# Layer A's sums of squares in a two-layer encoder: the additions move from GpSimd to VectorE

## The chip, the core and the metric

The kernel runs on one core of one Trainium2 chip. A core has five engines with instruction queues of their own: TensorE (PE in the profile; PEld is its weight load), VectorE (DVE), ScalarE (ACT), GpSimd (POOL) and SyncE (SP, which issues transfers here). They share an on-chip memory of 128 partitions and wait for each other by semaphores. The metric is the device time of one execution in microseconds (us); less is better.

## The reference

Two encoder layers on 512 tokens of width 1024, all in float32. Layer A is attention in three dilated windows, layer B attention in a two-dimensional neighbourhood. Cut to what matters:

```python
def rms_norm(x, g):
    y = x * lax.rsqrt(jnp.mean(x * x, axis=-1, keepdims=True) + RMS_EPS)
    return y * g

def reference(x, norm_gain, ...):
    for i in range(2):                       # layer A, then layer B
        hn = rms_norm(x, norm_gain[i])
        y = mixer_a(hn, ...) if i == 0 else mixer_b(hn, ...)
        x = x + y

def mixer_a(hn, w_in, w_out, ...):           # mixer_b has the same frame
    proj = hn @ w_in                         # q, k, v of each head group, and a gate
    ...                                      # attention
    return (y * silu(gate)) @ w_out
```

The change touches one step of this: the mean of `x * x` over the 1024 features of each token, in layer A's `rms_norm`.

## The kernel before, in words

**Layout.** x is held turned over, features on partitions: `x_all` is 8 blocks of 128 features x 512 tokens. The sum of squares over the features of a token therefore has two steps: the eight squared blocks are added, element by element, into one tile `ssq` (128 x 512), and a matmul with a column of ones (`row_sums`, tile `pk`) adds over the partitions.

**Matmuls in three parts.** A float32 product is made of three matmuls in a faster 32-bit format. Each operand is split into a high half, rounded, and a low half, the rest. For a weight, `cast` makes `wh` on ScalarE from the loaded `wraw`, and `rest` makes `wl` = `wraw` - `wh` on VectorE or GpSimd; among the first weights all of these subtractions go to VectorE. For x, `norm` makes `hn_h` on ScalarE and `hn_l` on VectorE, for each of the eight blocks. `mm3` issues the three matmuls, with `hn_h` x `wh`, `hn_h` x `wl`, `hn_l` x `wh` in this order.

**The beginning.** The first projection of layer A (`project`, eight steps k, each of four token blocks by three matmuls) uses x times its gain alone; the division by each token's root mean square, which needs `ssq`, is put in later as a scale of the results. So while TensorE works through the eight steps, block by block, ScalarE and VectorE make `hn_h`, `hn_l`, `wh` and `wl` for each step, ScalarE squares each block (`square_a`: block 0 straight into `ssq`, blocks 1 to 7 into tiles `sqx`, four of them in turn), and GpSimd adds the seven `sqx` to `ssq`, one after the other. After the first projection come the four small matmuls of `row_sums`, a reciprocal root on VectorE into `rs_n`, and `spread`, which hands it to all partitions (tile `pa`); then x itself is scaled (`scale_x`) and split anew (`renorm`, odd blocks on GpSimd), and sums and differences of its blocks are made for later products (`mix`, tiles `mixed`, `mix_h`, `mix_l`).

**Layer B** has the same step in `square_b`, where the additions are made by VectorE.

**The order of the work.** TensorE's order is that in which the program is traced, and it is written by hand: a generator `main` issues the large products, a generator `side` the rest (`square_a` and `row_sums` among them), and `run` interleaves them by an estimate of the matmuls' time. The other engines' queues are ordered by a planner that simulates the program, except where an instruction is pinned to the traced order. The engines' wrapper `Ordered` pins all of them while `held[0]` is set; it is set from the end of the second projection (some 54 us into the span) to the last attention step of layer A. So the beginning, with the change in it, and most of layer B are the planner's. Each engine runs its own queue strictly in that order: an instruction that waits holds up those behind it.

The functions that the diff touches, and what calls them:

Of the kernel before, what the change touches and what calls it, by code (L numbers as in the profile page):

```python
# [46 lines left out]
def tile_hybrid_encoder(  # L47
# [49 lines left out]
    vec, act, pol, syn = (Ordered(e) for e in (nc.vector, nc.scalar, nc.gpsimd, nc.sync))  # L97
# [407 lines left out]
    def square_a(k):  # L505
        if k == 0:
            st["ssq"] = wk.tile([P, S], F32, tag="eg", name="ssq", bufs=1)
        sq = wk.tile([P, 512], F32, tag="p", name="sqx", bufs=PB) if k else st["ssq"]
        act.activation(sq, x_all[:, k, :], AF.Square)
        if k:  # L510
            pol.tensor_add(st["ssq"], st["ssq"], sq)

    def scale_x():

# [82 lines left out]
    st = {}  # L597
# [807 lines left out]
    def side():  # L1405
        for k in range(KT):
            norm(0, k, x_all[:, k, :])
            if k:
                square_a(k - 1)
            stamp["na", k] = 0  # L1410
            yield 1000
        square_a(KT - 1)
        yield 8000
        row_scale(row_sums(st.pop("ssq")))
# [120 lines left out]
```

## Time and profile before

| | |
|---|---|
| median of 3 runs | 846.02 us (844.99 to 846.65) |
| profiled execution, its own time | 846.23 us |
| its span, from the first to the last instruction | 844.3 us |
| granted TensorE clock, mean | 1.000 |
| PE / DVE / ACT / POOL busy | 827.9 / 632.8 / 507.7 / 292.0 us |
| moved by DMA | 131.97 MB, mean 156 GB/s |

In the rows of the profile, L85 is the line of the wrapper `Ordered`, through which nearly every instruction of VectorE, ScalarE and GpSimd is issued, and L324 that of `matmul`; operations are therefore told apart by their tiles, written `out<-in`. A row of the order of time gives the start and the length in us, the engine, the instruction, its tiles and shape, how many equal neighbours are merged in the row, and in brackets the idle time of the engine before it and what ended that. The length of merged rows runs from the start of the first to the end of the last.

### The profile page before, as it was taken

Reading aid. Unit: us, or ns where it says so; the run is one execution under the profiler, and the core shown is the slowest. Engines: PE = TensorE matmul, PEld = TensorE weight load, DVE = VectorE, ACT = ScalarE, POOL = GpSimd, SP = SyncE. Lnnn points to the kernel's source line nnn. Section 1 sums busy time; section 2 is a strip of 40 time slices with the busy share of each in tenths; the row PEclk is TensorE's granted clock in tenths of the full one; section 3 lists DMA queues with packets and bytes.
Section 4 is the critical chain, followed back from the end, with each engine's and each line's share of the span. In section 5 each row is a group of like instructions: output and inputs, shape, how many; then the busy total and the mean of one; then the engine's idle time right before and its main releaser. Section 6 shows DMA issues by size and latency. Waiting matters only on the chain.

```text
span 844.3 us, 18126 instructions
## 1 busy us (share of the span) xinstructions
PE 827.9 (98%) x6611; PEld 684.9 (81%) x6611; DVE 632.8 (75%) x1653; ACT 507.7 (60%) x1066; POOL 292.0 (35%) x259
## 2 busy tenths in 40 slices
PE   8999999999999999999999999999999999999998
PEld 6877878878877878878888887789998898889786
DVE  7899997897996886896796876466668767776742
ACT  7657766846846846747747738454546664666440
POOL 5042343543533533533533524213123222322201
PEclk9999999999999999999999999999999999999999
DMA  9426765676687776785676554473265456634212
GB/s 339 144 57 165 194 154 150 141 168 197 133 181 211 159 174 173 164 210 134 157 180 176 105 183 144 152 235 114 91 191 164 130 145 180 179 129 114 85 51 101
DMA packets 56169, 131.97 MB, mean 156 GB/s; under 512 B 7184, under 2 KB 24528, under 8 KB 55952
## 3 DMA queue, kind: packets, MB, share of 16 engines
q1 hardware_dynamic: 49456, 108.39, 41.8%
q0 software_dynamic: 6048, 22.02, 15.2%
q8 instruction: 52, 0.85, 0.4%
q10 hardware_dynamic: 576, 0.41, 0.2%
q14 instruction: 37, 0.30, 0.1%
HBM read 111.73 MB, written 11.72 MB: 146 GB/s over the span
## 4 chain that ended last, share of the span: by engine, by line
PE 76%; ACT 9%; DVE 8%; issue 3%; DMA 3%; POOL 1%; SPq 0%; DVEq 0%; ACTq 0%; POOLq 0%
PE acc L324 63%; PE log L324 5%; PE o L324 4%; ACT p L85 4%; PE tp L328 3%; DVE wl L85 2%; ACT wh L85 1%; DVE na L85 1%; DMA wraw<-in_w 1%; DVE rawq L85 1%; DMA yr<-y_d 1%; ACT rawk L85 1%; DVE gt L85 1%; DVE p L85 1%; DMA pt<-in_xt 1%
## 5 line engine op out<-in xcount | busy, mean ns | idle before, releaser
L85 POOL TENSOR_TENSOR wl<-wraw,wh 128x512 fp32r<-128x512 f32 (+1 forms) x153 | 198.2, 1296 | 434.5 <-PE acc L324 223.2
L85 ACT CAST wh<-wraw 128x512 fp32r<-128x512 f32 (+1 forms) x360 | 209.3, 593 | 194.1 <-PE acc L324 154.9
L85 DVE TENSOR_TENSOR wl<-wraw,wh 128x512 fp32r<-128x512 f32 (+1 forms) x207 | 158.3, 768 | 44.5 <-PE acc L324 33.4
L324 PE MATMUL acc<-wh,hn_h 128*128 128x384 f32 (+1 forms) x488 | 185.5, 380 | 2.9 <-DVE gt L85 1.7
L324 PE MATMUL acc<-wl,hn_h 128*128 128x384 f32 (+1 forms) x488 | 177.2, 363 | 3.1 <-DVE wl L85 3.1
L324 PE MATMUL acc<-wh,hn_l 128*128 128x384 f32 (+1 forms) x488 | 176.9, 362 | 0.0
L85 ACT ACTIVATE p<-p,mn 128x256 f32<-128x256 f32 (+2 forms) x248 | 137.6, 584 | 32.3 <-DVE mn L85 32.3
L324 PEld LDWEIGHTS acc<-wh,hn_h 128*128 128x128 f32 x488 | 91.7, 188 | 21.4 <-issue 7.0
L324 PEld LDWEIGHTS acc<-wl,hn_h 128*128 128x128 f32 x488 | 91.9, 188 | 12.1 <-DVE wl L85 4.9
L324 PEld LDWEIGHTS acc<-wh,hn_l 128*128 128x128 f32 x488 | 91.6, 188 | 9.5
L324 PE MATMUL acc<-wh,mix_h 128*128 128x512 f32 x224 | 89.2, 398 | 0.0
L324 PE MATMUL acc<-wl,mix_h 128*128 128x512 f32 x224 | 87.6, 391 | 0.0
L324 PE MATMUL acc<-wh,mix_l 128*128 128x512 f32 x224 | 87.4, 390 | 0.0
L324 PE MATMUL acc<-hn_h,wh 128*128 128x512 f32 x192 | 79.0, 412 | 0.3 <-ACT rawb L85 0.2
L324 PE MATMUL acc<-hn_h,wl 128*128 128x512 f32 x192 | 75.1, 391 | 0.0
L324 PE MATMUL acc<-hn_l,wh 128*128 128x512 f32 x192 | 75.0, 391 | 0.0
L85 DVE STREAM_TRANSPOSE pt<-p 128x512 f32<-128x512 f32 (+1 forms) x60 | 40.6, 687 | 23.7 <-ACT p L85 23.6
L85 DVE TENSOR_REDUCE ss<-sq 128x4 f32<-128x256 f32 (+1 forms) x96 | 46.1, 501 | 11.0 <-POOL sq L85 5.9
L324 PE MATMUL acc<-y_h,wh 128*128 128x512 f32 x128 | 51.9, 406 | 0.5 <-ACT gt L85 0.5
L324 PEld LDWEIGHTS acc<-wh,mix_h 128*128 128x128 f32 x224 | 42.1, 188 | 10.0 <-issue 1.6
L324 PE MATMUL acc<-y_h,wl 128*128 128x512 f32 x128 | 50.0, 391 | 0.0
L324 PE MATMUL acc<-y_l,wh 128*128 128x512 f32 x128 | 49.9, 390 | 0.0
(148 smaller groups left out, 1361.5 us busy)
## 6 DMA issues: line engine op xcount, KB each, us to landing
wraw<-in_w SPq DMA_DIRECT2D x95, 512.0 KB
wraw<-in_w POOLq DMA_DIRECT2D x42, 512.0 KB, 7.0
wraw<-in_w SPq DMA_DIRECT2D x38, 384.0 KB
pt<-pt SPq DMA_DIRECT2D x106, 64.0 KB
td<-tr SPq DMA_DIRECT2D x24, 224.0 KB
pt<-td SPq DMA_DIRECT2D x24, 224.0 KB
e<-l_d SPq DMA_DIRECT2D x32, 112.0 KB
e<-l_d SPq DMA_DIRECT2D x16, 128.0 KB
```

The costliest lines, as they stand in the source:

```text
L85: m = f(*args, **kw)
L324: nc.tensor.matmul(o, l, r, **kw)
L328: nc.tensor.transpose(o, i, ident)
```

## The change

The addition of each squared block to `ssq` is issued on VectorE instead of GpSimd, seven times in all, on tiles of 128 x 512 in float32. Squares, tiles and the matmuls that read `ssq` stay as they are.

```diff
     def square_a(k):
         if k == 0:
             st["ssq"] = wk.tile([P, S], F32, tag="eg", name="ssq", bufs=1)
         sq = wk.tile([P, 512], F32, tag="p", name="sqx", bufs=PB) if k else st["ssq"]
         act.activation(sq, x_all[:, k, :], AF.Square)
         if k:
-            pol.tensor_add(st["ssq"], st["ssq"], sq)
+            vec.tensor_add(st["ssq"], st["ssq"], sq)
```

## The prediction

> **What bounds the kernel now.** I read the page first, then what TensorE waits for, then busy time by stretch, and last the order of time of each engine around the seven additions. From the page, the span, two engines' busy time and the chain that ended last:
>
> ```profile
> span 844.3 us, 18126 instructions
> PE 827.9 (98%) x6611; PEld 684.9 (81%) x6611; DVE 632.8 (75%) x1653; ACT 507.7 (60%) x1066; POOL 292.0 (35%) x259
> PE 76%; ACT 9%; DVE 8%; issue 3%; DMA 3%; POOL 1%; SPq 0%; DVEq 0%; ACTq 0%; POOLq 0%
> ```
>
> TensorE (PE) is busy for 98% of the span and carries 76% of the chain. So the time is the length of a matmul stream in a fixed order, plus the places where it stands still, and an edit on another engine counts only where it opens or closes such a place. The view of who waited for whom, TensorE's rows, names the largest kind (columns: us in total, times, longest):
>
> ```profile
> PE acc L324 <- DVE wl L85: 3.1, 3, 1.3
> ```
>
> `wl` is the low half of a weight, which VectorE (DVE) makes. Where these waits fall, and what VectorE and GpSimd (POOL) do there, is told by the busy time in three stretches (columns: stretch, its length, then busy us of PE, PEld, DVE, ACT, POOL with counts, granted clock, DMA share, GB/s):
>
> ```profile
> 8.40:20.70 12.30, 11.24 (x48) 8.42 (x47) 11.98 (x9) 11.08 (x20) 10.63 (x7) 1.00 1.03 410
> 20.70:27.00 6.30, 6.30 (x29) 5.22 (x28) 4.99 (x8) 1.25 (x2) 0.01 (x1) 1.00 0.79 238
> 27.00:54.00 27.00, 27.00 (x126) 21.42 (x126) 24.32 (x52) 16.72 (x29) 6.39 (x5) 1.00 0.38 100
> ```
>
> In the first stretch, where the additions run, VectorE is busy for 11.98 of 12.30 us with only 9 instructions; in the second, with GpSimd silent, it makes 8 in 4.99. The clock is 1.00 in all three. The two engines in order of time (start, length, instruction, count; neighbours of one kind are merged):
>
> ```profile
> 7.28 0.75 DVE L85 SCALAR_TENSOR_TENSOR hn_l<-pt,ng,hn_h 128x512 fp32r<-128x512 f32 x1 [0.41 <-ACT hn_h L85]
> 8.31 1.43 DVE L85 TENSOR_TENSOR wl<-wraw,wh 128x512 fp32r<-128x512 f32 x1 [0.28 <-ACT wh L85]
> 9.66 1.40 DVE L85 SCALAR_TENSOR_TENSOR hn_l<-pt,ng,hn_h 128x512 fp32r<-128x512 f32 x2
> 11.38 3.09 DVE L85 TENSOR_TENSOR wl<-wraw,wh 128x512 fp32r<-128x512 f32 x2 [0.32 <-ACT wh L85]
> 14.39 3.48 DVE L85 SCALAR_TENSOR_TENSOR hn_l<-pt,ng,hn_h 128x512 fp32r<-128x512 f32 x2
> 17.80 3.46 DVE L85 TENSOR_TENSOR wl<-wraw,wh 128x512 fp32r<-128x512 f32 x2
> 21.19 1.40 DVE L85 SCALAR_TENSOR_TENSOR hn_l<-pt,ng,hn_h 128x512 fp32r<-128x512 f32 x2
> 22.51 3.23 DVE L85 TENSOR_TENSOR wl<-wraw,wh 128x512 fp32r<-128x512 f32 x5
> ```
>
> ```profile
> 7.84 1.34 POOL L85 TENSOR_TENSOR ssq<-ssq,sqx 128x512 f32<-128x512 f32 x1 [6.53 <-ACT sqx L85]
> 10.46 10.25 POOL L85 TENSOR_TENSOR ssq<-ssq,sqx 128x512 f32<-128x512 f32 x6 [1.27 <-ACT sqx L85]
> 38.45 1.31 POOL L85 TENSOR_TENSOR hn_l<-pt,hn_h 128x512 fp32r<-128x512 f32 x1 [17.74 <-ACT hn_h L85]
> ```
>
> This is the heart of the case. The same `wl` operation costs 3.23 / 5 = 0.65 us after 22.51 and 3.46 / 2 = 1.73 us at 17.80. `hn_l` costs 1.40 / 2 = 0.70 us at 9.66 and 21.19, and 3.48 / 2 = 1.74 us at 14.39. The slow ones lie exactly where GpSimd's six additions lie, 10.46 to 20.71, and those come every 10.25 / 6 = 1.71 us, against 1.31 us for a GpSimd operation of that size at 38.45. The two engines step in turn, one operation each per 1.7 us. What that does to TensorE is in its own rows:
>
> ```profile
> 9.54 0.39 PE L324 MATMUL acc<-wh,hn_h 128*128 128x512 f32 x1
> 9.79 0.50 PE L324 MATMUL acc<-wl,hn_h 128*128 128x512 f32 x1
> 10.13 0.40 PE L324 MATMUL acc<-wh,hn_l 128*128 128x512 f32 x1
> ...
> 12.46 0.39 PE L324 MATMUL acc<-wh,hn_h 128*128 128x512 f32 x1
> 12.83 0.50 PE L324 MATMUL acc<-wl,hn_h 128*128 128x512 f32 x1
> 13.16 0.39 PE L324 MATMUL acc<-wh,hn_l 128*128 128x512 f32 x1
> 13.39 0.40 PE L324 MATMUL acc<-wh,hn_h 128*128 128x512 f32 x1
> ...
> 17.95 0.39 PE L324 MATMUL acc<-wh,hn_l 128*128 128x512 f32 x1
> 18.18 0.39 PE L324 MATMUL acc<-wh,hn_h 128*128 128x512 f32 x1
> 19.63 0.50 PE L324 MATMUL acc<-wl,hn_h 128*128 128x512 f32 x1 [1.06 <-DVE wl L85]
> 19.97 0.40 PE L324 MATMUL acc<-wh,hn_l 128*128 128x512 f32 x1
> ```
>
> Undisturbed, matmuls start 0.23 us apart (17.95 to 18.18, 13.16 to 13.39). Three times the one that first reads a new `wl` starts late: by 0.02 at 9.79, 0.14 at 12.83 and 1.22 at 19.63. After each the next comes 0.33 to 0.34 us on, 0.10 to 0.11 more than usual, so a halt costs a tenth on top. The three together: 0.02 + 0.14 + 1.22 + 3 x 0.11 = 1.7 us.
>
> **Taken away: seven additions on GpSimd.** They cost nothing directly, since nobody waits for GpSimd here; what goes is the slowing of VectorE. Over the seven VectorE operations that ran slow (one from 8.31, two each from 11.38, 14.39 and 17.80) that is 1.43 + 3.09 + 3.48 + 3.46 = 11.46 us, against five at 0.65 and two at 0.70 = 4.65 us: 6.8 us of VectorE's time.
>
> **Added: seven additions on VectorE.** This operation stands in the trace, since layer B adds its squares on VectorE already (min/median/max ns):
>
> ```profile
> L85 DVE TENSOR_TENSOR ssq<-ssq,sqx x7: 676/681/884, 569.2 to 576.5; 128x512 f32<-128x512 f32 x7
> ```
>
> Bounds: 0.65 us apiece by the row at 22.51, 0.88 by this row's longest. I take 0.68, the median: 7 x 0.68 = 4.8 us. So VectorE is left 6.8 - 4.8 = 2.0 us ahead when the stretch ends, while doing more.
>
> The additions are new waits in VectorE's queue: each waits for a square from ScalarE (ACT), and behind it are queued the `wl` and `hn_l` pieces that TensorE needs. Here is when squares and casts come:
>
> ```profile
> 8.46 1.34 ACT L85 ACTIVATE hn_h<-pt,ng 128x512 fp32r<-128x512 f32 x2 [0.18 <-DMA pt<-in_xt]
> 9.70 1.14 ACT L85 ACTIVATE sqx<-pt 128x512 f32<-128x512 f32 x2
> 10.74 1.12 ACT L85 CAST wh<-wraw 128x512 fp32r<-128x512 f32 x2
> 11.77 1.33 ACT L85 ACTIVATE hn_h<-pt,ng 128x512 fp32r<-128x512 f32 x2
> 13.01 1.14 ACT L85 ACTIVATE sqx<-pt 128x512 f32<-128x512 f32 x2
> 14.06 1.12 ACT L85 CAST wh<-wraw 128x512 fp32r<-128x512 f32 x2
> ```
>
> ScalarE makes squares before the casts of the same pair, so I take it that an addition is queued ahead of the `wl` of its pair. Walking VectorE with 0.65 for `wl`, 0.70 for `hn_l` and 0.68 for an addition: addition 1 from 8.0 (the `hn_l` of 7.28 ends), `wl` 1 to 9.3 (it was 9.74), `hn_l` 2 and 3 to 10.7, additions 2 and 3 to 12.1 (squares there by 10.84), `wl` 2 to 12.7 and `wl` 3 to 13.4, `hn_l` 4 and 5 to 14.8 (inputs by 13.10), additions 4 and 5 to 16.1 (squares by 14.15), `wl` 4 to 16.8. TensorE asks for `wl` 1 at 9.77: that halt goes. It asks for `wl` 2 at 12.69 less the 0.13 won before, so at 12.56: 0.14 late again, and the second halt, with its tenth 0.25 us, may stay. It asks for `wl` 4 at 18.41, or 18.0 when the earlier halts go: it has been there for over 1 us, so the largest halt goes, 1.22 + 0.11 = 1.33 us. Additions 6 and 7 end before 21, and who waits for them comes much later:
>
> ```profile
> 27.06 0.50 PE L324 MATMUL pk<-one,ssq 128*128 128x1 f32 x4
> ```
>
> TensorE reads the finished sum only at 27.06, or 25.4 in a stream ahead by 1.7. The cover is over 4 us; gone, every us of lateness would halt TensorE one to one.
>
> **The sum.** Gain 1.33 + 0.13 = 1.5 us with the second halt kept and 1.7 without; I take 1.6. After 20 us TensorE runs without idle time to 54 (27.00 of 27.00 us in the third stretch), and what VectorE does from 28 on starts from the matmul at 27.06, so all should move forward together. The profiled execution took 846.23 us, 1.9 above its span, and 846.23 - 1.6 = 844.6; against the median of 846.02 that is 844.4 us, or 0.19% less. A measurement of this kernel can tell about 0.2% from no change, 1.7 us here, so the forecast lies just at that line.
>
> **Rules weighed.** For the pace of 1.7 us: the Trainium skill, SBUF — State Buffer, "Who interferes with whom", says that a VectorE instruction with two SBUF inputs and a GpSimd one that reads SBUF exclude each other, the later blocking until the other's whole instruction is over. By it a pair would take 1.31 + 0.65 = 1.96 us where the trace shows 1.71, so the exclusion is seen, but not for quite the whole instruction. A rule that speaks against the change is in the Trainium skill, Perfetto Trace Analysis, "Optimizing Scalar/DVE Operations": where VectorE is saturated, moving work off it, even to GpSimd, may pay, though it adds that the shared port may spoil this. What it would do here is the first rival.
>
> **Rival 1, slower: VectorE is full and the additions lengthen its queue.** Place: the `wl` of 17.80. If the 1.7 us were the operations' own at that stage, additions 2 to 5 would put 4 x 0.68 = 2.7 us ahead of that `wl`, and TensorE's halt would grow by as much: 846.0 + 2.7 = 848.7 us. For it speaks 11.98 of 12.30 us busy; against it, the return to 0.65 as soon as GpSimd is silent, at the same granted clock. It decides at 0.91 us per operation: `wl` 4 ends nine operations behind 11.38 (`wl` 2 and 3, `hn_l` 4 and 5, four additions, itself), and 11.38 + 9 x 0.91 = 19.57 is where it ended. Chance 0.05.
>
> **Rival 2, slower: the planner orders the rest otherwise.** Orders on VectorE and ScalarE are computed up to about 54 us, and again in layer B; seven instructions on another engine can reshuffle them. The price of one bad place is in these rows:
>
> ```profile
> 71.71 1.23 DVE L85 TENSOR_TENSOR mix_l<-mixed,mix_h 128x1024 fp32r<-128x1024 f32 x1 [0.45 <-ACT mix_h L85]
> 73.59 0.50 PE L324 MATMUL acc<-wl,hn_h 128*128 128x512 f32 x1 [1.31 <-DVE wl L85]
> ```
>
> A `wl` behind a 1024-wide operation halts TensorE by 1.3 us. Two new such places turn 844.4 into 847.0; one leaves 845.7. VectorE's 24.32 of 27.00 us speaks for it; that most of the queues are pinned, against it. Chance 0.17 for two or more, 0.10 for one. A reshuffle that helps by as much, 1.3 us, would give 843.1; chance 0.08.
>
> **Rival 3, no change: the lead is lost at the next halt.** The wait of 1.31 us at 73.59 could grow by 1.6 if VectorE's work before it were tied to landings from HBM. Then 846.0. The DMA share of 0.38 speaks against it. Chance 0.10.
>
> **How the numbers follow.** The forecast, a gain of 1.5 to 1.7 carried through, has 0.50; with the spread of a measurement it splits, 0.33 beyond 0.2% and 0.17 short of it. Faster: 0.33 + 0.08 (helpful reshuffle) = 0.41. Slower: 0.05 + 0.17 = 0.22. Within: 0.17 + 0.10 + 0.10 = 0.37. The range reaches from 842.6 (helpful reshuffle, less 0.5 for the measurement) to 847.5 (two bad places, plus 0.5), leaving out rival 1 and worse reshuffles. The forecast's own range is 843.8 to 845.0.
>
> **What would show it.** Right: VectorE's `wl` and `hn_l` between 8 and 21 us at 0.65 to 0.75 us each; no wait near 19.6; the first matmul of `pk` at 25.4 to 25.6; the wait near 72 as long as before. Wrong: slow `wl` with GpSimd silent (rival 1), new `wl` waits of TensorE after 28 us (rival 2), or a longer wait near 72 with `pk` early (rival 3).

## The result, and the profile after

The changed kernel is slower: 850.37 us median of 9 runs (846.15 to 851.47), against 845.9 us for the kernel before in the 9 runs beside them (844.55 to 847.87). The ratio is 1.0034, with a 95% interval of 1.0019 to 1.0050; it is less than that of the two medians (1.0053) because the nine times fall into two groups, 846.15 to 848.1 and 850.37 to 851.47 us, and their median lies in the upper one. The forecast was 844.4 us and its range ended at 847.5. The profiled execution is one of the quickest of the nine, at 847.06 us, so its trace shows less of the loss than the median has. Its page has this to set against the three lines of before:

```profile
span 844.8 us, 18120 instructions
PE 830.0 (98%) x6611; PEld 686.6 (81%) x6611; DVE 630.7 (75%) x1660; ACT 507.8 (60%) x1066; POOL 281.9 (33%) x252
```

VectorE has the seven additions more and GpSimd the seven fewer, and VectorE's busy time falls by 2.1 us all the same. The operations themselves stand in the same order as before on every engine, apart from those seven; only the number of waits in the queues differs (two fewer on ScalarE, six fewer on GpSimd, one more each on VectorE and TensorE). That difference will matter.

**The beginning went as forecast on VectorE.** Busy time by stretch, after (columns as in the prediction), and VectorE in order of time:

```profile
8.40:20.70 12.30, 12.30 (x50) 10.05 (x49) 11.28 (x19) 11.18 (x20) 0.00 (x0) 1.00 1.03 411
```

```profile
11.00 1.49 DVE L85 TENSOR_TENSOR ssq<-ssq,sqx 128x512 f32<-128x512 f32 x2
12.40 1.29 DVE L85 TENSOR_TENSOR wl<-wraw,wh 128x512 fp32r<-128x512 f32 x2
13.61 1.41 DVE L85 SCALAR_TENSOR_TENSOR hn_l<-pt,ng,hn_h 128x512 fp32r<-128x512 f32 x2
...
15.54 0.68 DVE L85 TENSOR_TENSOR wl<-wraw,wh 128x512 fp32r<-128x512 f32 x1
...
17.34 1.41 DVE L85 SCALAR_TENSOR_TENSOR hn_l<-pt,ng,hn_h 128x512 fp32r<-128x512 f32 x2
...
20.48 0.68 DVE L85 TENSOR_TENSOR ssq<-ssq,sqx 128x512 f32<-128x512 f32 x1
```

TensorE has no idle time left here (12.30 of 12.30 us, 11.24 before; 12.28 in e11 below, where the clock came early). The clock column says 1.00 here, but the clock's record begins only at 10.88 us in this execution, and the view takes the time ahead of it as full. VectorE's `wl` takes 0.65 to 0.68 us and `hn_l` 0.71, where they took 1.73, and the `wl` that ended at 19.57 before is done by 16.22. The last `hn_l` ends at 18.75 us (22.59 before), with two additions still to come, so VectorE is 3.84 - 2 x 0.68 = 2.5 us ahead. The halts of 9.79 and 19.63 are gone.

**And yet `pk` came no earlier in this execution.** TensorE in order of time, after:

```profile
7.54 0.63 PE L324 MATMUL acc<-wh,hn_l 128*128 128x512 f32 x1
7.97 0.63 PE L324 MATMUL acc<-wh,hn_h 128*128 128x512 f32 x1
...
10.53 0.56 PE L324 MATMUL acc<-wh,hn_h 128*128 128x512 f32 x1
10.93 0.39 PE L324 MATMUL acc<-wl,hn_h 128*128 128x512 f32 x1
11.16 0.39 PE L324 MATMUL acc<-wh,hn_l 128*128 128x512 f32 x1
...
27.07 0.28 PE L324 MATMUL pk<-one,ssq 128*128 128x1 f32 x2
```

`pk` starts at 27.07 (27.06 before). Up to 10.9 us the matmuls come 0.43 us apart (7.54 to 7.97), and after that 0.23: the full clock is on record from 10.88 us, some 5 us later than in the profiled execution of before (5.69 us), whose matmuls were 0.23 us apart from 7.25 on. The eight steps from 7.54 to 10.93 took 3.39 us instead of 8 x 0.23 = 1.84, and these 1.5 us were the lead.

**Later something new appears.** Who waited for whom, TensorE's rows, after:

```profile
PE acc L324 <- DVE wl L85: 1.7, 2, 1.3
...
PE log L324 <- ACT k L85: 1.2, 2, 0.7
```

The first row had 3.1 us before and lost the halt of the beginning, as meant. The second has its two waits at 450 us:

```profile
450.34 0.38 PE L324 MATMUL log<-k0h,q0h 64*128 64x256 f32 x1 [0.45 <-ACT k L85]
451.43 0.39 PE L324 MATMUL log<-k0h,q0h 64*128 64x256 f32 x1 [0.72 <-ACT k L85]
```

The kernel before has no wait of TensorE there. Pairing the matmuls of two traces in order gives how far each execution is behind (+) or ahead (-) of the profiled execution of before, in us, at eight of its times. The labels are those of the experiments below:

```
before's time             27     72    262    268    448    455    630    830
after                  +0.01  +0.02  -0.02  -0.50  -0.48  +1.32  +0.50  +0.52
e1  after              -1.23  -1.22  -1.37  +0.93  +0.96  +3.33  +3.93  +3.94
e10 after              -0.10  -0.09  -0.21  -0.30  +0.10  +4.33  +4.81  +4.91
e11 after              -1.42  -1.41  -1.56  -0.50  -0.50  +3.07  +3.10  +3.14
e3  after, fillers     -1.38  -1.37  -1.56  -1.35  -1.38  +1.04  +1.65  +1.69
e6  before, nudged     +0.08  +0.07  -0.28  +0.13  -0.06  +3.04  +3.03  +3.19
e5  after, pad 2       +0.01  +0.01  -0.26  +0.46  +0.19  +1.00  +0.53  +0.64
e9  after, pad 1       -1.04  -1.02  -0.83  -0.77  -0.63  -0.63  -2.29  -2.30
e7  after, pad, fill   -1.14  -1.12  -1.29  -1.64  -1.80  -1.83  -2.61  -2.55
e12 after, pad, fill   -1.36  -1.38  -1.57  -2.31  -2.31  -2.34  -1.90  -1.86
e2  before             -0.37  -0.36  -0.45  -0.22  -0.07  -0.05  -1.07  -0.99
e4  before, fillers    -0.02  -0.01  -0.08  +0.17  +0.57  +0.57  +0.19  +0.26
e8  before, pad 2      +0.41  +0.39  +0.14  +0.51  +0.40  +0.37  -1.43  -1.33
```

The lead of 1.0 to 1.4 us is there at 27 where the clock came early, and it carries to 262. At 450 every traced execution of the changed kernel as it is falls back by 1.8 to 4.2 us. That is the loss, 400 us behind the edit. What is gained between 455 and 630 can't be put down to an edit: the unedited kernel before gains 1.0 us there too (e2).

**Where the 450 us wait comes from.** Followed back in order of time, these are rows of ScalarE, VectorE, GpSimd and SyncE. First the kernel before:

```profile
398.74 0.12 DVE L85 RECIPROCAL mn<-mn 128x1 f32<-128x1 f32 x1
398.96 0.72 ACT L85 ACTIVATE p<-p,mn 128x512 f32<-128x512 f32 x1 [0.27 <-DVE mn L85]
403.48 0.69 DVE L85 TENSOR_TENSOR wl<-wraw,wh 128x512 fp32r<-128x512 f32 x1
403.74 1.60 POOL L85 TENSOR_TENSOR wl<-wraw,wh 128x512 fp32r<-128x512 f32 x1
410.93 2.48 SPq L85 DMA_DIRECT2D pt<-pt  x4
429.90 7.43 SPq L85 DMA_DIRECT2D wraw<-in_w  x1
445.09 0.62 ACT L85 CAST wh<-wraw 128x512 fp32r<-128x512 f32 x1 [3.99 <-DMA wraw<-in_w]
```

The same places in the changed kernel:

```profile
398.25 0.12 DVE L85 RECIPROCAL mn<-mn 128x1 f32<-128x1 f32 x1
398.74 0.72 ACT L85 ACTIVATE p<-p,mn 128x512 f32<-128x512 f32 x1 [0.55 <-DVE mn L85]
403.27 2.40 DVE L85 TENSOR_TENSOR wl<-wraw,wh 128x512 fp32r<-128x512 f32 x1
403.52 1.59 POOL L85 TENSOR_TENSOR wl<-wraw,wh 128x512 fp32r<-128x512 f32 x1
412.43 1.85 SPq L85 DMA_DIRECT2D pt<-pt  x3
433.02 4.76 SPq L85 DMA_DIRECT2D wraw<-in_w  x1
446.43 0.62 ACT L85 CAST wh<-wraw 128x512 fp32r<-128x512 f32 x1 [5.81 <-DMA wraw<-in_w]
```

Before, ScalarE's normalising step `p<-p,mn` starts 0.10 us behind the end of the reciprocal that it waits for (398.86 to 398.96). After, it starts 0.37 us behind it (398.37 to 398.74), with nothing else to wait for. Then a `wl` on VectorE takes 2.40 us instead of 0.69. SyncE's issue of `pt` follows 1.5 us later (412.43, 410.93), and those behind it in its queue later still, the last weight's by 3.1 us (433.02, 429.90). ScalarE's cast of that weight comes 1.3 us later, the copies of `k` stand behind it, and TensorE waits for them. The chain that ended last, between 425 and 453 us, goes through TensorE alone before; in the changed kernel it leaves TensorE at this place for ScalarE:

```profile
449.10 0.60 ACT wh L85
449.70 0.58 ACT k L85
450.29 0.51 ACT wh L85
450.79 0.60 ACT k L85
451.39 0.04 issue
451.43 1.58 PE log L324 x58
```

**Why ScalarE stops for 0.3 us.** Counting all entries of ScalarE's queue from zero, waits included, this step is entry 703 in the changed kernel and 705 before, since two waits fell away. Elsewhere ScalarE stops for about as long, with everything that it waits for long done, at entries 63, 191, 319 and 1087, in one kernel or another. All of them are 63 more than a multiple of 128, and so is 703. No other place has such a stop: of the 1065 operations that ScalarE has in every one of the fourteen traces, thirteen stand still for at least 0.18 us more than in the median trace, and they are entries 63 and 703 in after, e1, e3, e10 and e11, 191 and 319 in e9, and 1087 in e8. The theory to test was therefore: the change moves ScalarE's later entries by two places, and this puts a stop that comes at fixed places of the queue onto a step of the critical kind. The rival: the loss is one of the clock alone, which comes late at the start and falls later whenever TensorE halts.

### The profile page after: what moved, and what is told of

It reads as the page before. It is cut to its first block, busy times and chain, and to the rows that moved or that the text cites. A ratio compares the mean times of both kernels' runs of the same rounds, so it can differ in the third digit from the quotient of the medians.

```text
span 844.8 us, 18120 instructions
## 1 busy us (share of the span) xinstructions
PE 830.0 (98%) x6611; PEld 686.6 (81%) x6611; DVE 630.7 (75%) x1660; ACT 507.8 (60%) x1066; POOL 281.9 (33%) x252
## 4 chain that ended last, share of the span: by engine, by line
PE 77%; ACT 8%; DVE 8%; DMA 3%; issue 3%; POOL 1%; ACTq 0%; DVEq 0%; SPq 0%
PE acc L324 64%; PE log L324 5%; PE o L324 4%; ACT p L85 4%; PE tp L328 3%; DVE wl L85 2%; ACT wh L85 1%; DVE na L85 1%; DMA wraw<-in_w 1%; DMA yr<-y_d 1%; DVE rawq L85 1%; ACT rawk L85 1%; DVE p L85 1%; DVE gt L85 1%; DVE tr L85 1%
## 5 line engine op out<-in xcount | busy, mean ns | idle before, releaser
L85 DVE TENSOR_TENSOR wl<-wraw,wh 128x512 fp32r<-128x512 f32 (+1 forms) x207 | 156.0, 756 | 45.2 <-PE acc L324 36.6
```

The lines of the kernel that those rows point to most:

```text
L85: m = f(*args, **kw)
```

## The experiments

**e1, e10 and e11: the changed kernel again, unedited.** Three more traces of it, to see which of the things above are always there.

> The changed kernel once more, for the spread of its times and the granted clock of each execution. In its profile the halts at 9.79, 12.83 and 19.63 us are gone, yet the small matmul that reads the finished sum starts at 27.07 us against 27.06 before, because the clock record reaches 1.0 only at 10.88 us (5.69 before) and ten matmuls run 0.43 us apart. Theory C (clock): the time depends on when the clock comes up and whether it falls again; executions with a mean clock of 0.999 or 1.0 come out at 845 to 848 us, those at 0.995 to 0.998 at 850 to 851.5, and a profile in which the clock is up by 5.7 us has the small matmul at 25.4. Theory L (later work): the change costs some 3 us somewhere after 28 us whatever the clock; then profiles show TensorE losing time there at a clock of 1.0, and slow executions have the same clock as fast ones.

> Changed kernel once more for a third profile. In its executions the mean clock is 0.998 or below in 8 of 14, against 5 of 59 of the kernel before in the shared runs. Theory P with a clock that falls: the long wait of TensorE at 450 us (2.4 us within 3.4 us) makes the clock fall to half for 3.41 us in some executions, 1.7 us more; a profile with a mean clock of 0.998 shows a stretch of 0.5 beginning between 450 and 456 us. Otherwise: the stretch lies at the start or at 264, where the kernel before has the same waits.

> The same for a fourth profile: always the 0.3 us stop at ScalarE's number 703, the 2.4 us piece at 403 and waits of 1.1 us or more at 450; the place where the clock falls, if it does, as in the run before it.

e1: 849.73 us (848.96 to 850.48, 5 runs), ratio 1.0040, interval 1.0027 to 1.0053. Two of its executions, 848.96 and 849.45 us, had a mean clock of 1.000, for which the clock theory allows 848 at most. The two single executions: 851.45 us (e10) and 849.68 us (e11). The expectation of e10 counts 5 of 59 executions of before at a mean clock of 0.998 or less; on record are 7 of 59. The step at entry 703 starts late, the slow `wl` and the waits for `k` are there in all four traces of this kernel. `pk` starts at 25.83 us in e1, at 26.96 in e10 and at 25.64 in e11: early where the full clock was there by 5.3 us, late where it came at 10.5. So the start varies, and a loss at 450 is always there. In e10 the clock also falls behind the two waits. TensorE in order of time, and busy time by stretch (the clock is the third column from the end), e10:

```profile
451.87 0.38 PE L324 MATMUL log<-k0h,q0h 64*128 64x256 f32 x1 [1.40 <-ACT k L85]
452.96 0.39 PE L324 MATMUL log<-k0h,q0h 64*128 64x256 f32 x1 [0.71 <-ACT k L85]
```

```profile
450.00:454.25 4.25, 2.13 (x65) 1.63 (x71) 3.09 (x6) 3.39 (x7) 1.57 (x1) 1.00 0.10 41
454.25:457.66 3.41, 3.41 (x38) 2.44 (x23) 2.06 (x11) 0.62 (x1) 1.42 (x2) 0.50 0.02 5
```

TensorE stood for half of the 4.25 us, and then had half a clock for 3.41 us, which by this count costs 3.41 x 0.5 = 1.7 us more. In e11 the same stretch lies at 452.39 to 455.80, in e1 at 263.97 to 267.39 behind a wait for `k` at 262. The trace agrees with the Trainium skill, TensorE: Matmul & The Clock Gate, "What's actually happening", that the clock is granted by windows of 3.4 us that do not start with the kernel: the full clock of e10 lasted from 10.52 to 454.25 us, 130 times 3.413, and in e11 it began at 5.24. It differs where that page of the Trainium skill asks for an idle window of that length before the clock falls, since here two waits of 1.40 and 0.71 us were enough, and in e11 0.74 and 0.72. Such waits do not always do it: in e6 below, 1.68 and 0.72 us at this place left the clock at 1.00.

**e2: the kernel before again, unedited**, to see how far one kernel differs from itself.

> The kernel before as a run of its own, for the granted clock of each execution, which the shared runs do not list. Theory C: its executions too differ in when the clock comes up, but a late clock costs it little, since the halt of 1.2 us at 19.6 swallows up to that much lateness; 844.5 to 848 us, and the mean clock stays at 0.999 or above in nearly all. Theory L says nothing of it beyond the ratio being 1.000.

845.7 us (844.92 to 847.88, 11 runs), ratio 0.9990 (0.9979 to 1.0001). The halt near 19 us is there, none at 450. `pk` starts at 26.69 us. A tenth of a per cent is what such a comparison can be off.

**e3 and e4: twelve filler matmuls instead of nine at the start, on the kernel after and on the one before.** They fill the idle stretch near 6 us, so that the clock is up by 7.0 us in every trace of such a kernel.

```diff
     busy = bank("busy")
-    for _ in range(9):
+    for _ in range(12):
         nc.tensor.matmul(busy, ones[:, :P], ones, start=True, stop=True)
```

> Changed kernel with 12 instead of 9 filler matmuls at the start, so that TensorE has no idle stretch between 5.7 and 6.9 us, where it waits for the first low half of a weight anyway. Theory C: the clock record reaches 1.0 by 8.3 us at the latest in every execution, few or no matmuls run at half rate, and the kernel is faster than the kernel before by 1.0 to 1.7 us (844.3 to 845), with fewer executions at 850. Theory L: the same 850 as the changed kernel.

> Kernel before with the same 12 filler matmuls. Theory C: its halts at 12.8 and 19.6 stay, an early clock only makes TensorE wait longer there: 845.5 to 846, within 0.1% of the kernel before. If it gains as much as the changed kernel does from the filler, the filler does something else than theory C says.

e3: 847.78 us (844.78 to 849.69, 12 runs), ratio 1.0014 (1.0000 to 1.0028). `pk` starts at 25.68, a lead of 1.4 us, and the waits at 450 are still there (1.08 + 0.71 us). e4: 845.12 us (844.58 to 846.51, 11 runs), ratio 0.9987 (0.9979 to 0.9996), its halt near 19.7 us unchanged (1.03 us of idle time, 1.06 in before) and `pk` at 27.03. So an early clock lets the lead show, is worth about a tenth of a per cent without the change too, and does not take the loss away. Both times miss what was expected: e3 lies between the two theories, with 1.2 us more than the kernel before, which is about the sum of the lead and of the 2.4 us lost at 450; e4 lies 0.4 us below its range. The clock alone is not the cause.

**e5 and e8: two more entries at the head of ScalarE's queue**, on the kernel after, which brings its later entries back to where they were before (the step is number 705 again), and on the kernel before as a control.

```diff
-    act.activation(warm, warm, AF.Exp)
+    for _ in range(3):
+        act.activation(warm, warm, AF.Exp)
```

> Changed kernel with two more tiny activations on ScalarE at the start, while it is idle. ScalarE's queue in the changed kernel holds two instructions fewer than before (two waits on GpSimd went), and in both its profiles ScalarE stands still for 0.32 us at its instruction number 703, and for 0.35 us at number 63, 640 = 5 x 128 later, with everything it waits for long done; in the kernel before no such stop is seen. Theory P (position): a stop of 0.3 us occurs where the queue passes a certain place every 128 instructions, unless the instruction there waits anyway; at 703 it falls on an operation that VectorE needs, VectorE's next weight piece (at 403 us) then comes behind GpSimd's instead of ahead of it and takes 2.40 instead of 0.69 us, SyncE's transfers are issued 1.5 us later, a weight lands late and TensorE loses 1.1 to 2.4 us at 450. With the two added back the stop leaves that operation: no 2.40 us piece at 403, no wait of TensorE at 450, and the time falls from about 850 to 844.5 to 846.5. Rival D (density): the early lead of 1 us itself changes what collides later; then the two activations change nothing and the time stays at 849 to 850.

> Kernel before with the two tiny activations, a control for their own cost: by theory P they are free at the start but move the places of the stops by two instructions, which may uncover one; within 0.15% of the kernel before unless the profile shows a new stop of 0.3 us on ScalarE with a wait of TensorE behind it. Rival D: unchanged.

e5: 846.43 us (843.8 to 847.56, 12 runs), ratio 0.9999 (0.9989 to 1.0009). The loss is gone with an edit of one line that adds work. The step at 399.22 us follows its reciprocal by 0.09 us, and the `wl` is quick:

```profile
399.22 0.72 ACT L85 ACTIVATE p<-p,mn 128x512 f32<-128x512 f32 x1 [0.27 <-DVE mn L85]
403.75 0.69 DVE L85 TENSOR_TENSOR wl<-wraw,wh 128x512 fp32r<-128x512 f32 x1
```

One wait for `k` of 0.48 us was left at 451 (the weight behind it, though issued at 429.73 us, landed only at 446.07), and the lead did not show since this execution had half a clock from 7.87 to 11.29 us. The control e8: 845.9 us (843.82 to 849.02, 12 runs), ratio 0.9998 (0.9985 to 1.0010), so the two entries gain nothing by themselves. In its trace the clock came as late as in that of after, at 10.79 us, and `pk` started at 27.47, 0.4 later than in the trace of before: in the kernel before most of a late start is swallowed by the halt at 19.63, where the kernel after has nothing that swallows it.

**e6: the kernel before, with the normalising step pushed late by two tiny copies on ScalarE.** Nothing of the change is in it.

```diff
         vec.reciprocal(mn[:, 3:4], mn[:, 2:3])
+        counted[0] += 1
+        if counted[0] == 44:
+            act.copy(warm, mn[:, 3:4])
+            act.copy(warm, warm)
         act.activation(pr, pr, AF.Copy, scale=mn[:, 3:4])
```

> Kernel before with two tiny copies (about 0.3 us together) on ScalarE just ahead of the normalising operation at 398.96 us, the one that stops in the changed kernel. Theory P: the same 0.3 us at the same place does the same there: VectorE's piece at 403 takes about 2.4 us, TensorE waits 1 to 3 us at 450, and the kernel before becomes slower by 1 to 2.5 us (847.5 to 849) with no edit to its beginning. Rival D: 0.3 us of ScalarE in the middle is covered, time unchanged.

849.6 us (847.17 to 851.06, 7 runs), ratio 1.0039 (1.0025 to 1.0054): the whole loss of the change, without the change. Its ScalarE, VectorE and TensorE in order of time:

```profile
398.85 0.19 ACT L85 COPY warm<-mn 128x1 f32<-128x1 f32 x1 [0.21 <-DVE mn L85]
399.17 0.72 ACT L85 ACTIVATE p<-p,mn 128x512 f32<-128x512 f32 x1
403.69 2.40 DVE L85 TENSOR_TENSOR wl<-wraw,wh 128x512 fp32r<-128x512 f32 x1
452.09 0.38 PE L324 MATMUL log<-k0h,q0h 64*128 64x256 f32 x1 [1.68 <-ACT k L85]
453.19 0.38 PE L324 MATMUL log<-k0h,q0h 64*128 64x256 f32 x1 [0.72 <-ACT k L85]
```

The step starts 0.36 us behind the end of its reciprocal (398.81 us), where it had 0.10 in before and 0.37 in after. So 0.26 us of lateness at this one step is enough for all that follows. The clock stays at 1.00 behind the two waits, so the 3.1 us lost here (-0.06 at 448, +3.04 at 455) owe nothing to it.

**e9: one more entry instead of two** (the loop of e5 with 2 in place of 3), which puts the step at entry 704 and other steps at places of the suspected kind.

> Changed kernel with one tiny activation more on ScalarE at the start instead of two. The place that stops at number 703 then meets the wait just ahead of the normalising operation, which starts 0.9 us after the operation before it and ends with the event it waits for. Theory P: the stop is hidden in that wait, so one instruction does as much as two: no 2.40 us piece at 403, TensorE does not wait at 450, time 845 to 847, against 849 to 850 for the changed kernel. If the number of the instructions were not what matters but the waits themselves, one would do nothing or half.

846.01 us (844.24 to 848.26, 12 runs), ratio 1.0006 (0.9997 to 1.0016). No slow `wl` near 403 and no wait at 450. The stop turns up elsewhere, at entry 191, the copy `vt` at 110 us, and TensorE's transposes wait longer for it. ScalarE and TensorE of e9:

```profile
110.14 1.06 ACT L85 COPY vt<-acc 128x512 f32<-128x512 f32 x1 [0.34 <-DVE ss L85]
111.54 0.44 PE L328 MATMUL tp<-ident,vt 128*128 128x128 f32 x2 [1.06 <-ACT vt L85]
```

TensorE of the kernel before:

```profile
112.27 0.33 PE L328 MATMUL tp<-ident,vt 128*128 128x128 f32 x1 [0.73 <-ACT vt L85]
```

1.06 against 0.73 us (0.73 to 0.82 in the other traces): a stop of 0.3 us passed on about one to one. One place in the queue decides which step is hit.

**e7 and e12: both edits together on the kernel after** (two more entries, twelve fillers), run twice.

> Changed kernel with both the two tiny activations and 12 filler matmuls. Theory P with an early clock: the predicted gain appears whole, 1.3 to 2 us faster than the kernel before (844 to 845). Rival D: as the changed kernel with 12 fillers alone, about 848.

> Changed kernel with two tiny activations and 12 fillers again, to narrow its ratio to the kernel before (0.9992, 0.9979 to 1.0004 so far). Theory P with an early clock: 0.998 to 0.9995, that is 0.5 to 1.7 us faster. If the gain at the start is given back later for another reason: 1.000.

e7: 845.0 us (843.13 to 848.37, 12 runs), ratio 0.9992 (0.9979 to 1.0004). e12: 844.66 us (844.08 to 846.6, 11 runs), ratio 0.9978 (0.9964 to 0.9991). The second is faster than the kernel before by its interval, the first only in its median, so the 1.3 to 2 us expected of it did not show; no edit of the study was quicker than e12. TensorE in e12:

```profile
25.69 0.28 PE L324 MATMUL pk<-one,ssq 128*128 128x1 f32 x2
```

The lead is there, nothing is lost at 450 (-2.31 at 448, -2.34 at 455 in the table), and the clock stays at 1.00. Since e4 has 0.9987 without the change, the change's own share of this gain is about a tenth of a per cent or less, which these runs can't separate.

**How often the clock falls.** An execution's mean granted clock is at or below 0.998 when it has had at least one such half-clock stretch (3.41 x 0.5 / 845 = 0.002); a clock that comes late at the start is not in this mean. That holds for 20 of 35 executions of the kernels that have the stall at 450 us (after, e1, e3, e6, e10, e11), and for 17 of 163 of all others. In the nine times of after, the five with 0.998 or less are 850.37 to 851.47 us, the four others 846.15 to 848.1. The count doesn't tell where the stretch lies: in the traces of the first group it lies behind the waits at 450 in e10 and e11, at 264 us in e1 and at 7.87 in e6, and after and e3 have none. The clock adds to the loss; it doesn't start it.

## Why the prediction was wrong

**What bounds the kernel: right.** The time is TensorE's stream plus its halts, and both gain and loss came as halts.

**The cost of the seven additions: right.** The group of all additions to `ssq` on VectorE, those of layer B among them, in the changed kernel (count, then busy us, mean ns of one, and idle time before them):

```profile
L85 DVE TENSOR_TENSOR ssq<-ssq,sqx 128x512 f32<-128x512 f32 x14 | 9.8, 700 | 0.8 <-ACT sqx L85 0.5
```

0.70 us apiece in the group, and 0.68 to 0.69 for the seven that moved, against 0.68 forecast; VectorE is 2.5 us ahead against 2.0.

**The three halts: right in kind, with 1.0 to 1.4 us instead of 1.6.** With the clock up early `pk` starts at 25.64 to 26.02 us (e1, e3, e7, e9, e11, e12), where 25.4 to 25.6 was forecast. The halts at 9.79 and 19.63 are gone. The one at 12.83, which was left open, stays in these traces, 0.2 to 0.7 us late.

**The clock at the start: a step that was missing.** The prediction took 1.00 in all three stretches, which is what one profiled execution had. The full clock was granted between 4.5 and 10.9 us in the traces of this study. In two of the four traces of the unedited changed kernel it came at 10.5 us or later, and the lead at 27 us was 0.1 us or none.

**"So all should move forward together": the step that failed.** It rested on TensorE running without idle time to 54 us, and what came later was given one rival, a planner that orders the rest otherwise. No operation was reordered. What moved was two waits out of ScalarE's queue, because ScalarE no longer has to wait for GpSimd: where the prediction says that nobody waits for GpSimd here, ScalarE's queue held such waits, at the reuse of the `sqx` tiles and of the buffer of `ssq`. With them went the place in the queue of every later entry. One stop of 0.3 us then fell on a step whose lateness costs VectorE 1.7 us (2.40 - 0.69), SyncE's issues up to 3.1 us, and TensorE, at 450 us, 1.8 to 2.4 us with the clock kept (after, e1, e3) and up to 4.2 us with it lost (e10). With a lead of 1.4 us or none, this makes -1.4 + 2.4 = +1.0 to +4.2 us. The medians are 4.5 us up for after and 3.2 for e1; the execution of after with a mean clock of 0.995 lost at least 0.0045 x 848 = 3.8 us to the clock, so it had more than one half-clock stretch.

**The rivals.** Rival 1 did not happen: `wl` was quick as soon as GpSimd was silent. Rival 2 named the right effect on TensorE and about the right price (two halts, 2.6 us together, against 1.8 to 4.2 us at 450), but by a mechanism that isn't there; that the size fits is luck. Rival 3 expected the lead to be lost at the halt near 73 us; that one is 1.32 us in after and 1.31 before. None had an unchanged order with another timing, and so the range ended 3 us short.

**What is shown and what is not.** Shown: that the lateness of the one step makes the loss (e6), that moving ScalarE's entries by one or two places takes it away (e5, e9), that the clock alone neither makes nor cures it (e3 keeps the loss with an early clock, e5 lacks it with half a clock at 7.87 us), and that the stops stand at entries 63 more than a multiple of 128 (thirteen of thirteen). Inferred only: that they come there because instructions are fetched in blocks; no row of these traces names a releaser for them. The Trainium skill, Runtime: NRT & Kernel Launch, "Instruction fetch mechanics", has blocks of 256 instructions whose crossing is mostly hidden, which fits neither the spacing nor the 0.3 us seen here. Open: why the lateness makes just that `wl` slow. It ends 0.56 us after GpSimd's `wl` ends (403.27 + 2.40 against 403.52 + 1.59), about its own undisturbed length, which agrees with the exclusion that the Trainium skill, SBUF — State Buffer, "Who interferes with whom", states. But the recorded starts of the two are 0.25 us apart in the slow case and 0.26 in the quick one, so they don't tell why the other engine goes first. An experiment that keeps GpSimd out of that weight's `wl` was not tried. Open as well is the twin place at 262 us, where TensorE waits for `k` in some executions of all kinds of kernel, that of before among them (0.64 us at 263.56), and not in others.

## What to carry to other kernels

An edit that removes or adds waits, or instructions, moves every later entry of the queues that it touches, and a stop of a few tenths of a microsecond may land on a step that hands it to other engines: when a local gain is smaller than one such halt, compare the whole trace for the first place where the paired matmuls fall apart, not only the stage that was edited. A control that shifts the queue by one or two harmless entries tells a real cost of the change from a shifted stop. And a single profile has one clock history; a gain of two tenths of a per cent needs several.

## What the runs showed of the hardware

- ScalarE's queue stopped for about 0.3 us at entries 63, 191, 319, 703 and 1087 (0.55 instead of 0.27 us idle ahead of entry 703), all 128 or a multiple of it apart, and nowhere else in fourteen traces. Which of them cost anything depends on the step that stands there.
- Two waits of TensorE of 1.40 and 0.71 us, so close together that it stood for half of 4.25 us, were followed by 3.41 us at half the clock (e10); two of 1.68 and 0.72 us in e6 were not. Half-clock stretches were 3.41 to 3.42 us long wherever they were seen before the end, at 7.87 us (e5) and 264 us (e1) too.
- Three more filler matmuls, put where TensorE would have been idle near 6 us, brought the full clock by 7.0 us in all four traces that had them, where it came as late as 10.9 without; on the kernel before this gave 0.9987 (0.9979 to 0.9996).
- When two engines' subtractions on the same memory collide, one can take 2.40 instead of 0.69 us, and which one is decided by a shift of 0.2 to 0.3 us several microseconds earlier (after, e6).
